# The first ordinary slab of the next product, token block by token block inside the norm

## The chip, the cores and the metric

The kernel runs on one core of one Trainium2 chip. The metric is the device time of one launch in microseconds (us). A core has five engines with an instruction queue each: TensorE (PE, matrix products), VectorE (DVE), ScalarE (ACT), GpSimd (POOL), and SyncE (SP), which here only issues loads. Each engine takes its instructions in the order of its queue; between engines, semaphores order the work.

## The reference, cut to what matters

256 tokens of width 1024 pass through a chain of blocks in float32. After each block comes a residual and a layer norm, and the next block begins with a product of the normalized x:

```python
def first_block(x, mem, ...):
    ...
    y = jnp.concatenate([mix, mem_out], axis=-1) @ w_out
    x = layer_norm(DN_ALPHA * x + y, ln_mix_g, ln_mix_b)              # norm 1
    h = jnp.square(jax.nn.relu(x @ w_up))
    return layer_norm(DN_ALPHA * x + h @ w_down, ln_ffn_g, ln_ffn_b)  # norm 2

def second_block(x, ...):
    for i in range(2):                    # i = 0: mla, i = 1: hyena
        m = mla_mixer(x, ...) if i == 0 else hyena_mixer(x, ...)
        x = layer_norm_2(ALPHA * x + m, ln1_g[i], ln1_b[i])           # norms 3 and 5
        x = layer_norm_2(ALPHA * x + conv_ffn(x, ...), ln2_g[i], ln2_b[i])  # norm 4 and the last
    return x

def conv_ffn(x, w_up, w_conv, w_down):
    h = dwconv_centred(x @ w_up, w_conv)
    a, g = jnp.split(h, 2, axis=-1)
    return (jax.nn.silu(g) * a) @ w_down
```

`first_block` is followed by `second_block`. The products that follow the five inner norms are: x @ w_up (norm 1), x @ mla_w_in (norm 2), x @ ffn_w_up of layer 0 (norm 3), x @ hy_w_in (norm 4), x @ ffn_w_up of layer 1 (norm 5).

## The kernel before

**Numbers.** Every large product is computed from parts: an fp32 operand is a high part in fp32r plus a low part (the difference), and three products (high by high, high by low, low by high) are summed in PSUM. `split` (L65 to L68) makes the parts: ACT copies the high part, DVE subtracts. The lines that the profile shows for it are L67 (ACT) and L68 (DVE).

**Weights.** `weights` (from L75) loads a slab of 128 x 1024 numbers, 512 KB, from SP's queue (L82) into one of three raw buffers, `wraw`, and splits it into `whi` (ACT) and `wlo` (DVE), of which there are five pairs. A raw buffer is free again after its `wlo`. So a load starts when the wlo of the slab three loads earlier is done.

**A product of weights by x** yields columns on the partitions and the 256 tokens along the free axis. `gemm_b` (L102) takes 24 matmuls of 256 columns for a slab, 8 each for (whi, x high), (wlo, x high), (whi, x low). After norm 1, `gemm_wide` (L110, L112) takes 8 matmuls of 512 columns (x high and low side by side) and 8 of 256.

**The norm.** A block's last product is summed in four PSUM banks, `acc`: two token blocks of 128 tokens by two halves of 512 columns (L116 to L118). `Down.end` writes the transition out by hand for each norm. Its parts are: `tail(b)`, the last matmuls of token block b; `ln_block(b, ...)`, the norm of the block on DVE (L159 to L170, with one small step on POOL) followed by transposes of the normalized rows on TensorE (`ln_t`, L178) and the split of the result into `x` (ACT, then DVE); `first_mm(b, ...)`, the product of this token block with the next weights' first 512 columns (L199, 24 matmuls of 512 columns, out of the four slabs `first`), written out to `utok` by ACT (L201). Later `first_pair` transposes `utok` (L209, `f4t`).

The order written by hand is tail(0), the norm of block 0, the four slabs of the first columns, tail(1), first_mm(0), the norm of block 1, first_mm(1). After that, `norm["after"] = 6` makes the splits of the next six slabs (in `weights`) come no earlier than the last DVE instruction of block 1's norm. A scheduler then sets the order on each engine from this program order and its own estimates of when things are ready; the engines keep that order.

The next stage then begins with an ordinary slab: `ff1_mm(4)`, `c_mm(4)`, `up(2)` (twice) or `hy_mm(4)`. It is followed by the products already at hand in `utok`.

**Side work.** During the first feed-forward stage `rope_tables` loads `posi` and casts it on DVE. During the first conv_ffn stage `hyena_filter` loads `f_wfb`, combines it on POOL into `f_wpm`, which ACT and DVE split into `f_wh` and `f_wl`.

Of the kernel before, what the change touches and what calls it, by code (L numbers as in the profile page):

```python
# [18 lines left out]
P = 128  # L19
# [24 lines left out]
def block_kernel(ctx, tc, A, out, taps=None):  # L44
# [11 lines left out]
    def bank(name="ps"):  # L56
        return psp.tile([P, 512], F32, name=name, tag="ps")
# [130 lines left out]
    def first_mm(b, x, ws, utok):  # L188
# [11 lines left out]
                             start=i == 0, stop=i == len(seq) - 1)  # L200
        nc.scalar.activation(utok[:, b, :], ps, AF.Copy)  # L201

    def first_pair(utok, i, ps=None):

        ps = bank("f4t") if ps is None else ps
        for j in range(2):
            for b in range(2):
                c = (2 * i + j) * P
                nc.tensor.transpose(ps[:, j * S + b * P:j * S + (b + 1) * P], utok[:, b, c:c + P], ident)  # L209
        return ps[:, :S], ps[:, S:]  # L210
# [3 lines left out]
    class Down:  # L214
# [21 lines left out]
                for i, (act, w) in enumerate(self.pend):  # L236
                    gemm_a(self.acc, b, h, act, w, False, i == len(self.pend) - 1)

        def end(self, gb, alpha, first, room=None):
            last = first is None  # L240
            x = utok = ws = None
            self.tail(0)
            if not last:
                x = new_x()
                utok = lnp.tile([P, 2, 512], F32, name="utok", tag="utok")
            ln_block(0, self.acc, x, gb, alpha, last)
            if not last:
                room = room or [None] * 4
                ws = [weights(first[i], room[i]) for i in range(4)]
            self.tail(1)  # L250
            if not last:
                first_mm(0, x, ws, utok)
            with tc.issue_after(norm["inst"].ins):
                ln_block(1, self.acc, x, gb, alpha, last)
            if not last:
                first_mm(1, x, ws, utok)
                norm["after"] = 6
            return x, utok

    def spare(pool, tags):  # L260

# [253 lines left out]
    pipeline([Stick(p) for p in range(SB_PAIRS)] + [Mem(p, b) for p in range(2) for b in range(2)], filler)  # L515
    for k in range(4, 8):
        u_dn(k)
    x, utok = dn.end(gb, ALPHA_1, A["w_up_f"], spare(p1, F4_TAGS))
    ph.close()
    tap("t_mix")  # L520

# [72 lines left out]
        nc.vector.tensor_copy(f_hl[0:64], hx[0:64].bitcast(F32))  # L594

    mlp = filter_mlp()
    ready = [ff1_act(ff1_mm(4))]
    order = [4, 0, 1, 2, 3] + list(range(5, FF1_TILES))
    for i in range(2):
        for ps in first_pair(utok, i):  # L600
# [1 line left out]
    for i in range(FF1_TILES):  # L602
# [4 lines left out]
            rope_tables()  # L607
        if i >= 6 and i % 4 == 2:
            next(mlp, None)
    x, utok = dn.end(gb, ALPHA_1, A["mla_w_in_f"], spare(p2, F4_TAGS))  # L610
    ph.close()
    tap("t_ffn")

# [29 lines left out]
        nc.vector.scalar_tensor_tensor(cl[:, nt, :], ps, gqk[:, nt:nt + 1], ch[:, nt, :].bitcast(F32),  # L643
                                       op0=ALU.mult, op1=ALU.subtract)

    c4 = c_mm(4)
    fp = [ps for i in range(2) for ps in first_pair(utok, i)]
    for j in range(3):
        c_act(j, fp[j])
# [125 lines left out]
    pipeline([Latent(h) for h in range(MLA_HEADS)], filler)  # L775
    for k in range(4, 8):
        u_wo(k)
    x, utok = dn.end(gb, ALPHA_2, A["ffn_w_up_f"][0], spare(p3, F4_TAGS))
    ph.close()
    rs.close()  # L780
    tap("t_mla")
# [82 lines left out]
        return steps + [(load_dft, "c_inv1"), (load_dft, "c_inv2")]  # L864


    def conv_ffn(layer, x, utok, nxt, side):
        with ExitStack() as es:
            pf = es.enter_context(tc.tile_pool(name=f"pf{layer}", bufs=1))
            todo = side(es.enter_context(tc.tile_pool(name="flt", bufs=1))) if side else []  # L870
            per = -(-len(todo) // (FF2_TILES - 5))
            wc = lnp.tile([P, 2 * FF2_TILES, 3], F32, name="wc", tag="wc")
            nc.sync.dma_start(wc, A["ffn_w_conv"][layer])
            gb = ln_load(pf, A["ln2_g"][layer], A["ln2_b"][layer])
            dn = Down(FF2_TILES, TAIL if nxt is not None else SPLIT_BUFS)

            def mm(nt):
                w = weights(A["ffn_w_up"][layer, nt])
                ps = bank("up")
                gemm_b(ps[:, :S], w, 0, x, KT)  # L880
                return ps[:, :S]

            def act(j, pss):
                ts = []
                for i in range(2):
                    t = pf.tile([P, S], F32, name=f"t{i}", tag=f"t{i}", bufs=2)
                    dwconv(t, pss[i], wc[:, j + i * FF2_TILES, :])
                    ts.append(t)
                ta, tg = ts
                nc.scalar.activation(tg, tg, AF.Silu)  # L890
                nc.vector.tensor_tensor(ta, ta, tg, op=ALU.mult)
                return act_split(pf, ta, "h", 5)

            def up(j):
                return act(j, [mm(2 * (j - 2) + i) for i in range(2)])

            ready = [up(2)]
            ready += [act(j, first_pair(utok, j)) for j in range(2)]
            order = [2, 0, 1] + list(range(3, FF2_TILES))
            for i in range(FF2_TILES):  # L900
                if i + 3 < FF2_TILES:
                    ready.append(up(i + 3))
                dn.add(ready[i], A["ffn_w_down"][layer, order[i]])
                if i:
                    for f, *a in todo[(i - 1) * per:i * per]:
                        f(*a)
            return dn.end(gb, ALPHA_2, nxt)

    x, utok = conv_ffn(0, x, utok, A["hy_w_in_f"], hyena_filter)
    tap("t_l0")  # L910


# [301 lines left out]
```

## Time and profile before

| what | us |
| --- | --- |
| median of 3 runs | 965.04 |
| lowest and highest run | 963.87, 969.01 |
| the profiled execution | 964.65 |
| its span in the trace | 962.9 |

The granted TensorE clock of the profiled execution is 0.992 on average. The table of the span in 40 slices shows the busy share in tenths:

```profile
PE   9999999999999999999999999998989999999996
DVE  6887679777667879779889788889779878777776
ACT  4676636454445577556666566445675355555551
```

TensorE is near full almost everywhere, DVE around three quarters, ACT about half. Times in the timeline are microseconds from the span's start; a row gives start, duration, engine, line, operation, out<-in, shapes, the count, and in brackets the idle time before it and what ended it. The five norms lie at about 122 to 141, 308 to 327, 400 to 419, 612 to 634 and 757 to 777 us.

### The profile page before, as it was taken

To read this page: it belongs to the slowest core of one execution; us is meant where nothing else is said; L and a number is where in the kernel's file an instruction comes from. 1 tells how busy PE (TensorE), PEld (TensorE's weight loads), DVE (VectorE), ACT (ScalarE), POOL (GpSimd) and SP (SyncE) were. 2 spreads that over 40 slices of the span, in tenths; PEclk is the share of its full clock that TensorE was granted. 3 is DMA by queue.
4 is the path that set the end of the run, shared out by engine and by line. 5 is a ranking of instruction groups with operands and counts; after the bars stand their busy time and mean duration, and the time that the engine had idled before them with its cause. 6 is when DMAs were issued, how large, how long until landed. Compare 5 with 4: busy or idle time off the path is not lost.

```text
span 962.9 us, 15208 instructions
## 1 busy us (share of the span) xinstructions
PE 932.9 (97%) x5808; PEld 823.7 (86%) x5808; DVE 761.1 (79%) x1201; ACT 539.9 (56%) x878; POOL 64.0 (7%) x61
## 2 busy tenths in 40 slices
PE   9999999999999999999999999998989999999996
PEld 6889788888887898788899999888978799999995
DVE  6887679777667879779889788889779878777776
ACT  4676636454445577556666566445675355555551
POOL 0000000000000010011312211001210000000000
PEclk9999999999999999999999999999989999999999
DMA  7764536655665443576555556436995565555551
GB/s 248 261 198 132 166 117 223 204 175 181 192 193 193 160 126 109 176 248 220 184 170 177 176 182 198 153 98 159 262 242 144 173 231 184 181 192 185 186 177 44
DMA packets 51082, 173.83 MB, mean 181 GB/s; under 512 B 6236, under 2 KB 7101, under 8 KB 50881
## 3 DMA queue, kind: packets, MB, share of 16 engines
q1 hardware_dynamic: 48656, 164.34, 52.6%
q0 software_dynamic: 2352, 8.52, 4.6%
q8 instruction: 46, 0.75, 0.3%
q14 instruction: 28, 0.22, 0.1%
HBM read 171.13 MB, written 1.05 MB: 179 GB/s over the span
## 4 chain that ended last, share of the span: by engine, by line
PE 75%; DVE 11%; DMA 7%; ACT 4%; issue 2%; SPq 0%; DVEq 0%; ACTq 0%; POOLq 0%
PE up L102 23%; PE acc L116 9%; PE acc L117 9%; PE acc L118 9%; PE up L110 5%; PE f L199 5%; DVE wlo L68 3%; PE up L112 3%; PE proj L102 2%; DMA wraw<-w_v 1%; ACT whi L67 1%; DMA wraw<-hy_w_in 1%; DMA wraw<-ffn_w_up_f 1%; PE hin L102 1%; DMA wraw<-w_qk 1%
## 5 line engine op out<-in xcount | busy, mean ns | idle before, releaser
L68 DVE TENSOR_TENSOR wlo<-wraw,whi 128x1024 fp32r<-128x1024 f32 (+1 forms) x255 | 310.4, 1220 | 78.4 <-ACT whi L67 77.5
L67 ACT ACTIVATE whi<-wraw 128x1024 fp32r<-128x1024 f32 (+1 forms) x255 | 265.2, 1044 | 128.1 <-PE acc L117 45.8
L102 PE MATMUL up<-x,whi 128*128 128x256 f32 x1280 | 173.7, 283 | 2.0 <-DVE t L790 2.0
L102 PEld LDWEIGHTS up<-x,whi 128*128 128x128 f32 x1280 | 164.8, 191 | 6.2 <-ACT whi L67 2.1
L118 PE MATMUL acc<-wlo,hh 128*128 128x512 f32 x304 | 119.9, 396 | 0.0
L116 PE MATMUL acc<-whi,hh 128*128 128x512 f32 x304 | 119.9, 396 | 0.0
L117 PE MATMUL acc<-whi,hl 128*128 128x512 f32 x304 | 119.9, 395 | 0.0
L102 PE MATMUL up<-x,wlo 128*128 128x256 f32 x640 | 89.8, 283 | 0.0
L787 ACT ACTIVATE t<-up,wc 128x256 f32<-128x256 f32 x80 | 37.7, 473 | 91.8 <-PE up L102 89.0
L102 PEld LDWEIGHTS up<-x,wlo 128*128 128x128 f32 x640 | 82.4, 192 | 0.0
L788 DVE SCALAR_TENSOR_TENSOR t<-up,wc,t 128x255 f32<-128x255 f32 x80 | 38.2, 479 | 46.3 <-ACT t L787 46.0
L118 PEld LDWEIGHTS acc<-wlo,hh 128*128 128x128 f32 x304 | 57.1, 188 | 13.5
L116 PEld LDWEIGHTS acc<-whi,hh 128*128 128x128 f32 x304 | 57.4, 189 | 11.3 <-ACT hh L67 0.5
L117 PEld LDWEIGHTS acc<-whi,hl 128*128 128x128 f32 x304 | 57.0, 188 | 11.0 <-DVE hl L68 0.3
L110 PE MATMUL up<-x,whi 128*128 128x512 f32 x224 | 56.6, 395 | 0.0
L165 POOL TENSOR_TENSOR ln_rs<-ln_rs,mhalf 128x1 f32<-128x1 f32 x12 | 11.5, 958 | 646.3 <-DVE ln_rs L164 646.3
L110 PEld LDWEIGHTS up<-x,whi 128*128 128x128 f32 x224 | 41.8, 188 | 10.6 <-issue 1.1
L102 PE MATMUL hin<-x,whi 128*128 128x256 f32 x320 | 46.7, 292 | 0.0
L102 PEld LDWEIGHTS hin<-x,whi 128*128 128x128 f32 x320 | 42.7, 199 | 0.3
L790 DVE SCALAR_TENSOR_TENSOR t<-up,wc,t 128x255 f32<-128x255 f32 x80 | 38.3, 480 | 2.1
L67 ACT ACTIVATE hh<-h 128x256 fp32r<-128x256 f32 x32 | 13.1, 415 | 39.1 <-DVE h L544 38.0
L112 PEld LDWEIGHTS up<-x,wlo 128*128 128x128 f32 x224 | 30.6, 190 | 2.3
(404 smaller groups left out, 1665.2 us busy)
## 6 DMA issues: line engine op xcount, KB each, us to landing
wraw<-ffn_w_up SPq DMA_DIRECT2D x80, 512.0 KB, 4.2
wraw<-ffn_w_down SPq DMA_DIRECT2D x44, 512.0 KB, 3.7
wraw<-w_down SPq DMA_DIRECT2D x32, 512.0 KB, 3.5
wraw<-w_up SPq DMA_DIRECT2D x28, 512.0 KB, 4.3
wraw<-hy_w_in SPq DMA_DIRECT2D x20, 512.0 KB, 5.1
wraw<-w_qk SPq DMA_DIRECT2D x14, 512.0 KB, 4.5
wlo<-hy_w_in POOLq DMA_DIRECT2D x11, 512.0 KB, 9.4
wraw<-w_out SPq DMA_DIRECT2D x8, 512.0 KB, 3.4
```

Source lines behind the costliest of these rows:

```text
L67: nc.scalar.activation(hi, src, AF.Copy)
L68: nc.vector.tensor_tensor(lo, src, hi.bitcast(F32), op=ALU.subtract)
L102: nc.tensor.matmul(ps, a[:, off + k * P:off + (k + 1) * P], m[:, k, :], start=i == 0, stop=i == len(seq) - 1)
L110: nc.tensor.matmul(ps, wh[:, k * P:(k + 1) * P], xx[:, k], start=k == 0, stop=False)
L112: nc.tensor.matmul(ps[:, :S], wl[:, k * P:(k + 1) * P], xh[:, k, :], start=False, stop=k == KT - 1)
L116: nc.tensor.matmul(ps, ah, mh, start=start, stop=False)
L117: nc.tensor.matmul(ps, al, mh, start=False, stop=False)
L118: nc.tensor.matmul(ps, ah, ml, start=False, stop=stop)
L199: nc.tensor.matmul(ps, x[xi][:, k, tb], ws[k // 2][wi][:, o:o + 512], start=i == 0, stop=i == len(seq) - 1)
L787: norm["act"] = nc.scalar.activation(dst, ps, AF.Copy, scale=w3[:, 1:2])
L788: nc.vector.scalar_tensor_tensor(dst[:, 1:], ps[:, :S - 1], w3[:, 0:1], dst[:, 1:], op0=ALU.mult, op1=ALU.add)
L790: norm["dve"] = nc.vector.scalar_tensor_tensor(dst[:, :S - 1], ps[:, 1:S], w3[:, 2:3], dst[:, :S - 1], op0=ALU.mult, op1=ALU.add)
```

## The change

Each of the five callers hands `end` one more slab, `lead`: the one that its stage took first. `end` loads it right behind the four slabs of the first columns, and `lead_mm` multiplies it with one token block at a time, directly after `first_mm` of that block: 24 matmuls of 128 columns for block 0, ahead of block 1's transposes, and 24 for block 1. The result is one PSUM bank of 256 columns, `lead`, that the stage uses in place of its first product. The count of slabs whose splits are held back becomes 5, since one slab fewer follows. After norm 1, `ff1_act` gets a product of 256 columns in place of the wide one, and so takes its other branch.

```diff
+    def lead_mm(ps, b, x, w):
+        tb = slice(b * P, (b + 1) * P)
+        seq = [(w[i], x[j], k) for i, j in ((0, 0), (0, 1), (1, 0)) for k in range(KT)]
+        for i, (a, m, k) in enumerate(seq):
+            nc.tensor.matmul(ps[:, tb], a[:, k * P:(k + 1) * P], m[:, k, tb],
+                             start=i == 0, stop=i == len(seq) - 1)
...
-        def end(self, gb, alpha, first, room=None):
+        def end(self, gb, alpha, first, lead=None, room=None):
...
                 ws = [weights(first[i], room[i]) for i in range(4)]
+                lw = weights(lead)
             self.tail(1)
             if not last:
+                ps = bank("lead")
                 first_mm(0, x, ws, utok)
+                lead_mm(ps, 0, x, lw)
             with tc.issue_after(norm["inst"].ins):
                 ln_block(1, self.acc, x, gb, alpha, last)
             if not last:
                 first_mm(1, x, ws, utok)
-                norm["after"] = 6
-            return x, utok
+                lead_mm(ps, 1, x, lw)
+                norm["after"] = 5
+                ps = ps[:, :S]
+            return x, utok, ps
...
-    x, utok = dn.end(gb, ALPHA_1, A["w_up_f"], spare(p1, F4_TAGS))
+    x, utok, lead = dn.end(gb, ALPHA_1, A["w_up_f"], A["w_up"][0], spare(p1, F4_TAGS))
-    ready = [ff1_act(ff1_mm(4))]
+    ready = [ff1_act(lead)]
...
-    x, utok = dn.end(gb, ALPHA_1, A["mla_w_in_f"], spare(p2, F4_TAGS))
+    x, utok, c4 = dn.end(gb, ALPHA_1, A["mla_w_in_f"], A["mla_w_in"][0], spare(p2, F4_TAGS))
-    c4 = c_mm(4)
...
-    x, utok = dn.end(gb, ALPHA_2, A["ffn_w_up_f"][0], spare(p3, F4_TAGS))
+    x, utok, lead = dn.end(gb, ALPHA_2, A["ffn_w_up_f"][0], A["ffn_w_up"][0, 0], spare(p3, F4_TAGS))
-            ready = [up(2)]
+            ready = [act(2, [lead, mm(1)])]
...
-            return dn.end(gb, ALPHA_2, nxt)
+            return dn.end(gb, ALPHA_2, nxt, nxt_lead)
...
-    va = [hy_mm(4)]
+    va = [lead]
```

The calls at norm 4 (`A["hy_w_in"][0]`) and norm 5 (`A["ffn_w_up"][1, 0]`) change in the same way.

How this moves instructions is shown at norm 1. On ACT, with the buffer numbers, before the change, from the last slab split ahead of the norm to the write of `utok` of block 1 (`x` from `ln_t_1423` and `ln_t_1431` is block 0, the next pair block 1):

```order
L67 ACTIVATE whi_1673<-wraw_1672 128x1024
L67 ACTIVATE x_1408<-ln_t_1423 128x4x128
L67 ACTIVATE x_1408<-ln_t_1431 128x4x128
L201 ACTIVATE utok_1409<-f4_1478 128x512
L67 ACTIVATE x_1408<-ln_t_1517 128x4x128
L67 ACTIVATE x_1408<-ln_t_1525 128x4x128
L67 ACTIVATE whi_1695<-wraw_1694 128x1024
L67 ACTIVATE whi_1726<-wraw_1725 128x1024
L201 ACTIVATE utok_1409<-f4_1532 128x512
```

And the same place of the changed kernel, where `wraw_1454` is lead's slab, loaded ahead of `wraw_1672`:

```order
L67 ACTIVATE whi_1704<-wraw_1703 128x1024
L67 ACTIVATE x_1408<-ln_t_1423 128x4x128
L67 ACTIVATE x_1408<-ln_t_1431 128x4x128
L67 ACTIVATE whi_1726<-wraw_1725 128x1024
L201 ACTIVATE utok_1409<-f4_1485 128x512
L67 ACTIVATE whi_1757<-wraw_1756 128x1024
L67 ACTIVATE x_1408<-ln_t_1548 128x4x128
L67 ACTIVATE x_1408<-ln_t_1556 128x4x128
L201 ACTIVATE utok_1409<-f4_1563 128x512
```

Two splits of slabs, 1726 and 1757, that stood behind x of block 1 now stand ahead of it. At norms 2 and 3 one such split does (`whi_3522` of w_uq_n, `whi_4656` of ffn_w_down); at norms 4 and 5 none stands between utok of block 0 and x of block 1.

On DVE, before the change, from the end of block 1's norm at norm 1 to the cast of `posi`:

```order
L170 SCALAR_TENSOR_TENSOR xt<-xt,ln_rs,ln_b 128x512 x2
L68 TENSOR_TENSOR wlo<-wraw,whi 128x1024 x2
L68 TENSOR_TENSOR x<-ln_t,x 128x4x128 x2
L68 TENSOR_TENSOR wlo<-wraw,whi 128x1024 x4
L543 TENSOR_TENSOR h<-up,h 128x256
L540 TENSOR_TENSOR h<-h 128x256
L544 SCALAR_TENSOR_TENSOR h<-h 128x256
L68 TENSOR_TENSOR hl<-h,hh 128x256 x2
L68 TENSOR_TENSOR wlo<-wraw,whi 128x1024
L540 TENSOR_TENSOR h<-h 128x256 x2
L68 TENSOR_TENSOR hl<-h,hh 128x256 x2
L558 CAST ang<-posi 128x256
```

And of the changed kernel:

```order
L170 SCALAR_TENSOR_TENSOR xt<-xt,ln_rs,ln_b 128x512 x2
L68 TENSOR_TENSOR wlo<-wraw,whi 128x1024 x4
L68 TENSOR_TENSOR x<-ln_t,x 128x4x128 x2
L571 CAST ang<-posi 128x256
L68 TENSOR_TENSOR wlo<-wraw,whi 128x1024
L553 TENSOR_TENSOR h<-h 128x256 x2
L572 TENSOR_SCALAR ang<-ang,invf 128x256
L68 TENSOR_TENSOR hl<-h,hh 128x256 x2
```

The cast moved ahead of the first h. On SP, the loads of this place before the change:

```order
L82 DMA wraw<-w_down 128x1024
L150 DMA ln_g<-ln_ffn_g 128x1024
L150 DMA ln_b<-ln_ffn_b 128x1024
L82 DMA wraw<-w_up 128x1024
L82 DMA wraw<-w_down 128x1024
L554 DMA posi<-positions 128x256
```

And of the changed kernel:

```order
L82 DMA wraw<-w_down 128x1024
L82 DMA wraw<-w_up 128x1024
L150 DMA ln_g<-ln_ffn_g 128x1024
L150 DMA ln_b<-ln_ffn_b 128x1024
L567 DMA posi<-positions 128x256
```

One slab more is issued ahead of ln_g, and posi follows ln_b directly.

More of the change, by code (lines that the diff above doesn't have):

```diff
@@ L237, in tail @@
                     gemm_a(self.acc, b, h, act, w, False, i == len(self.pend) - 1)
-        def end(self, gb, alpha, first, room=None):
+        def end(self, gb, alpha, first, lead=None, room=None):
             last = first is None
-            x = utok = ws = None
+            x = utok = ws = lw = ps = None
             self.tail(0)
@@ L864, in hyena_filter, with conv_ffn @@
         return steps + [(load_dft, "c_inv1"), (load_dft, "c_inv2")]
-    def conv_ffn(layer, x, utok, nxt, side):
+    def conv_ffn(layer, x, utok, lead, nxt, nxt_lead, side):
         with ExitStack() as es:
@@ L906, in conv_ffn @@
                         f(*a)
-            return dn.end(gb, ALPHA_2, nxt)
-    x, utok = conv_ffn(0, x, utok, A["hy_w_in_f"], hyena_filter)
+            return dn.end(gb, ALPHA_2, nxt, nxt_lead)
+    x, utok, lead = conv_ffn(0, x, utok, lead, A["hy_w_in_f"], A["hy_w_in"][0], hyena_filter)
     tap("t_l0")
@@ L1091, in block_kernel @@
     room = keep.tile([P, 4, 2, D], F32R, name="Kf", tag="Kf")
-    x, utok = dn.end(gb, ALPHA_2, A["ffn_w_up_f"][1], [(room[:, i, 0], room[:, i, 1]) for i in range(4)])
+    x, utok, lead = dn.end(gb, ALPHA_2, A["ffn_w_up_f"][1], A["ffn_w_up"][1, 0], [(room[:, i, 0], room[:, i, 1]) for i in range(4)])
     ph.close()
     tap("t_hy")
-    conv_ffn(1, x, utok, None, None)
+    conv_ffn(1, x, utok, lead, None, None, None)
 def _tiles(w):
```

## The prediction

> **What bounds the kernel now.** I read the head of the page first, then the table of what TensorE (PE) waited for, then busy time by stretch around the five norms.
>
> ```profile
> span 962.9 us, 15208 instructions
> PE 932.9 (97%) x5808; PEld 823.7 (86%) x5808; DVE 761.1 (79%) x1201; ACT 539.9 (56%) x878; POOL 64.0 (7%) x61
> ...
> PE ln_t L178 <- DVE xt L170: 2.1, 2, 1.1
> PE f L199 <- ACT x L67: 0.9, 3, 0.3
> ```
>
> TensorE is busy 97% of the span, so a microsecond that TensorE loses or gains counts nearly in full. At the norms it waits little: 2.1 us for the normalized rows and 0.9 us for the split of x (and once 0.7 us for utok, in a row further down). These 3.7 us are all that work put between the first columns and the transposes could fill.
>
> ```profile
> 128.00:150.00 22.00, 21.70 (x110) 18.09 (x109) 17.21 (x26) 8.56 (x16) 0.99 (x1) 1.00 0.53 187
> 312.00:331.00 19.00, 17.99 (x100) 15.01 (x101) 15.75 (x27) 8.31 (x19) 1.15 (x2) 1.00 0.33 110
> 331.00:403.00 72.00, 70.78 (x454) 62.94 (x453) 57.76 (x130) 50.39 (x106) 4.47 (x7) 1.00 0.51 161
> 403.00:433.00 30.00, 29.70 (x187) 26.32 (x186) 24.81 (x36) 15.35 (x24) 3.33 (x4) 1.00 0.58 196
> 618.00:640.00 22.00, 20.10 (x116) 16.82 (x116) 17.88 (x27) 9.25 (x13) 0.99 (x1) 1.00 0.46 142
> 640.00:763.00 123.00, 113.66 (x734) 102.94 (x733) 104.99 (x157) 73.42 (x108) 14.11 (x16) 0.96 0.74 197
> 763.00:785.00 22.00, 21.64 (x132) 18.54 (x131) 17.10 (x25) 8.88 (x13) 0.92 (x1) 1.00 0.48 164
> ```
>
> The columns are the window, its length, and busy time of PE, weight loads, DVE, ACT, POOL. The idle of PE (length less busy) is 0.3 us at norm 1, 1.0 at norm 2, 0.3 at norm 3, 1.9 at norm 4 (window from 618), 0.4 at norm 5; the stage after norm 2 has 1.2 and the hyena stage (640 to 763) 9.3.
>
> **The price of the matmuls.** The chain that ended last gives spacings:
>
> ```profile
> 141.37 1.85 PE up L110 x8
> 143.23 0.95 PE up L112 x8
> ...
> 327.19 2.88 PE c L102 x24
> ...
> 371.26 1.05 PE o L760 x4
> ```
>
> An fp32r matmul of 512 columns costs 231 ns (1.85 / 8), one of 256 columns 119 to 120 ns (0.95 / 8; 2.88 / 24). The product that the change replaces costs 2.8 us at norm 1 and 2.88 us at the others. In its place stand 2 x 24 matmuls of 128 columns. No fp32r matmul below 256 columns is in the trace. Lower bound: 60 ns, half of 120, if only columns count. Upper bound: 216 ns, the plain fp32 matmul of 256 columns (the row of o: 3 spacings and one duration of 0.386 us make 1.05). The nearest row of the same width is that of the fp32 transposes:
>
> ```profile
> 134.20 1.03 PE L178 MATMUL ln_t<-ident,xt 128*128 128x128 f32 x8
> 135.54 1.21 PE L199 MATMUL f<-f4h,x 128*128 128x512 f32 x4 [0.30 <-ACT x L67]
> ```
>
> Eight take 1.03 us with the last one's own 0.276 us, so (1.03 - 0.28) / 7 = 108 ns. I take 115 ns, between this and the 120 ns at 256 columns, which means that halving the columns gains nearly nothing while the weights are loaded anew each time. Then 24 cost 2.76 us, a norm's two 5.5 us, 2.7 us more than before.
>
> [...]
>
> **Norm 1: the split of block 1 comes behind a load.** The instruction order shows the main step. Before the change ACT does x (block 1) right after utok; now whi of raw 1756 stands between them. The three raw buffers go round: 1454 (lead), 1672, 1703, then 1725 in lead's buffer and 1756 in that of 1672, whose wlo is the first that DVE does after block 1's norm. So this load starts after the norm. These rows of ACT, DVE and SP of before show how long this takes:
>
> ```profile
> 134.89 1.08 ACT L67 ACTIVATE x<-ln_t 128x512 fp32r<-128x512 f32 x2
> 139.32 1.06 ACT L67 ACTIVATE whi<-wraw 128x1024 fp32r<-128x1024 f32 x1 [3.35 <-DMA wraw<-w_up]
> ...
> 132.24 1.41 DVE L170 SCALAR_TENSOR_TENSOR xt<-xt,ln_rs,ln_b 128x512 f32<-128x512 f32 x2
> 133.56 2.35 DVE L68 TENSOR_TENSOR wlo<-wraw,whi 128x1024 fp32r<-128x1024 f32 x2
> ...
> 134.85 0.33 SPq L82 DMA_DIRECT2D wraw<-w_up  x1
> ```
>
> The norm of block 1 ends at about 133.6, the first wlo at 134.8, SP issues the load at 134.85, and ACT can split it at 139.32; before, x was long done and this hurt nobody. Now the load in this slot is w_down, of the same size. x of block 1 starts at 139.32 + 1.06 = 140.4 and f of block 1, which started 0.65 us after x (134.89, 135.54), at 141.0: 5.4 us late. Behind the waiting whi on ACT stand both x and utok; TensorE has only lead(0) (2.8 us) and the transposes for that time, then idles about 2.5 us. lead(1) ends at 141.0 + 5.7 + 2.76 = 149.4, where up(4) ended at 144.0, so 5.4 us are lost by then. On DVE the added wlo inside block 0's norm (1.2 us) fits in an idle of the same size there; I cost it at nothing, and at 1.2 us if that cover is gone.
>
> Then a second one. The cast of posi moves on DVE from behind four hl to right behind x, ahead of the first h:
>
> ```profile
> 146.04 0.44 SPq L554 DMA_DIRECT2D posi<-positions  x1
> ...
> 151.74 0.30 DVE L558 CAST ang<-posi 128x256 f32<-128x256 int32 x1 [0.57 <-DMA posi<-positions]
> ...
> 147.71 0.39 PE L116 MATMUL acc<-whi,hh 128*128 128x512 f32 x1
> ```
>
> The load took 5.7 us. On SP it now stands behind the loads of ln_g and ln_b, which wait for the end of f of block 1 (146.6): issue about 147.7, landing 153.4. Behind the cast on DVE are wlo, h and hl, for which acc waits: 153.4 + 0.3 + 1.2 + 0.4, and the hi and lo parts, gives acc at about 155.7, where it began at 147.71. **Norm 1: +8.0 us.**
>
> **Norm 2**, the same trap:
>
> ```profile
> 312.95 0.63 PE L178 MATMUL ln_t<-ident,xt 128*128 128x128 f32 x4 [0.98 <-DVE xt L170]
> ...
> 320.44 1.22 DVE L68 TENSOR_TENSOR wlo<-wraw,whi 128x1024 fp32r<-128x1024 f32 x1
> ...
> 324.89 0.85 ACT L67 ACTIVATE whi<-wraw 128x768 fp32r<-128x768 f32 x1 [2.95 <-DMA wraw<-w_uq_r]
> ```
>
> Here lead's wlo inside block 0's norm is not hidden, since the transposes already waited 0.98 us for DVE: +1.2 us. The first wlo after block 1's norm moves from 320.44 to 321.7; 4.45 us after its start the loaded slab was split (324.89), so now at 326.1, for 0.85 us. f of block 1 starts at 327.6 instead of 321.32 (0.65 us after x). It ends at 333.4, lead(1) at 336.1; c ended at 327.19 + 2.88, about 329.9 with the overlap of the last. **+6.2 us.** lead(0), from 321.2, is hidden.
>
> **Norm 3**, the same again, with POOL behind it:
>
> ```profile
> 411.86 2.35 DVE L68 TENSOR_TENSOR wlo<-wraw,whi 128x1024 fp32r<-128x1024 f32 x2
> ...
> 413.05 1.08 ACT L67 ACTIVATE x<-ln_t 128x512 fp32r<-128x512 f32 x2
> 416.86 1.06 ACT L67 ACTIVATE whi<-wraw 128x1024 fp32r<-128x1024 f32 x1 [2.73 <-DMA wraw<-ffn_w_up]
> ...
> 432.33 0.64 ACT L67 ACTIVATE f_wh<-f_wpm 128x512 fp32r<-128x512 f32 x1 [0.76 <-POOL f_wpm L827]
> ...
> 434.57 0.63 ACT L67 ACTIVATE f_wh<-f_wpm 128x512 fp32r<-128x512 f32 x1 [1.30 <-POOL f_wpm L827]
> ...
> 439.59 1.19 PE L102 MATMUL up<-x,whi 128*128 128x256 f32 x8 [1.82 <-DVE t L790]
> ```
>
> The wlo moves from 411.86 to 413.1, the whi from 416.86 to 418.1, x to 419.2, f to 419.8, from 413.70 (413.05 + 0.65): 6.1 us; with the narrower product 6.2 at the end of lead(1). After that ACT has both f_wh ahead of t of the second product; their input comes from POOL at 432.3 and 434.6 before, and at about 433.8 and 436 now, since its load is issued about 1.4 us later. The t of the second product is then read at about 436.6, over 11 us later than before, its bank is not free, and acc begins some 4 us later than the 6.2 alone explain. Of this, 1.8 us come back, because the wait of 1.82 us at 439.59 came from the same filter work. **+8 us** (6.2 to 10).
>
> **Norm 4**: x of block 1 stands ahead of the late whi, so there is no trap.
>
> ```profile
> 625.74 0.44 PE L209 MATMUL f4t<-ident,utok 128*128 128x128 f32 x2 [0.69 <-ACT utok L201]
> 627.30 1.38 PE L178 MATMUL ln_t<-ident,xt 128*128 128x128 f32 x8 [1.12 <-DVE xt L170]
> ```
>
> lead(0) fills the two waits (1.8 us), but one more wlo stands ahead of block 1's norm on DVE, so the transposes go from 627.3 to 628.5. **+1.1 us** (1.2 and lead(1) for the old product, 2.76 for 2.88).
>
> **Norm 5**: no trap either (block 1's x comes first), but nothing hides: block 0's norm ended when the transposes began, so its added wlo costs 1.2 us.
>
> ```profile
> 761.98 1.41 DVE L170 SCALAR_TENSOR_TENSOR xt<-xt,ln_rs,spec_q 128x512 f32<-128x512 f32 x2
> ...
> 763.24 1.03 PE L178 MATMUL ln_t<-ident,xt 128*128 128x128 f32 x8
> ```
>
> With the 2.7 us of narrower matmuls, less 0.1: **+3.8 us.**
>
> Sum: 8.0 + 6.2 + 8.0 + 1.1 + 3.8 = 27.1; I take off 1 us for what the idle of 1.2 us after norm 2 gives back. 964.65 (the profiled execution: span 962.9 and 1.75 around it) + 26 = 990.7; the median of the runs is 0.4 above that execution: **991 us.**
>
> **Rivals.**
> - *The late whi costs less than its row.* If these loads land before the norm's end (another slot free sooner), f of block 1 starts on time, and what is left is the narrow matmuls and the wlo: norm 1 +2.7, norm 2 +3.9, norm 3 +3.3, norm 4 +1.1, norm 5 +3.8, or 980. For it: at 139.32 the wait was for a load, not for ACT. Against it: the load cannot start before its buffer is free. Chance 0.15.
> - *Later stages take it back.* The hyena stage has 9.3 us of idle PE, part of it for loads whose issue need not move with TensorE. If the stage starts 23 us late with weights landed, up to 9 us return: 982. Against it: its buffers are freed by the same delayed engines. Chance 0.12.
> - *The reordered hyena stage, or a matmul of up to 216 ns, costs more.* At 216 ns lead(1) costs 2.4 us more at each norm, and at norm 5 and part of norm 4 lead(0) too: about +15, or 1006. Chance 0.10.
> - *Faster than before.* The waits that work can fill are 1.8 us at norm 4 and about 0.4 elsewhere, 2.2 in all. They are a gain if the late whi and the added wlo hide entirely and a matmul of 128 columns takes less than 69 ns (5 x (48 x 0.069 - 2.88) = 2.2); at 60 ns the time is about 963. Below 960 there is nothing to gain. Chance 0.04.
> - *The narrow matmul is cheap.* At the lower bound of 60 ns the traps remain and lead(0) stays hidden at norms 1 to 4: lead(1) saves 24 x 0.055 = 1.3 us at five norms, lead(0) as much at norm 5, 983. For it: columns set the 231 and 120 ns. Against it: the 108 ns of the transposes. Chance 0.04. [...]
>
> The forecast keeps 0.55.
>
> **Range.** The forecast alone spans 983 to 999 (matmul at 60 to 120 ns, norm 3 at +6.2 to +10, the hyena stage by a few us). I reach below to the two cases of 980 and 982, with some for both together, and above toward 1006: 974 to 1003. A difference under 0.5% cannot be told from none for this kernel, by the spread of its runs. Slower by more than that 0.93, within it 0.04, faster 0.03.
>
> **What would show it.** A wait of f for ACT x of 2 us and more at norms 1, 2 and 3, and none at 4 and 5; on ACT a whi that waits some 3 us for its load right ahead of x of block 1; the lead rows at about 115 ns each; DVE waiting for posi ahead of the first h; acc 8 us late at norm 1. It is wrong if f of block 1 starts as promptly as before.

## The result, and the profile after

| what | us |
| --- | --- |
| after, median of 6 runs (lowest to highest) | 1004.42 (1000.72 to 1009.59) |
| before on the same chip, median of 6 runs | 964.45 |
| ratio, with its 95% interval | 1.041 (1.0383 to 1.0438) |
| the profiled execution after, and its span | 1004.86, 1003.1 |

The kernel became 40 us slower, where 26 were forecast; 1004.42 lies just above the range, which ended at 1003. The mean granted clock of the profiled execution is 0.981 (0.992 before).

The head of the page after, with the busy time by engine:

```profile
span 1003.1 us, 15462 instructions
PE 954.4 (95%) x5936; PEld 843.5 (84%) x5936; DVE 759.8 (76%) x1200; ACT 540.2 (54%) x878; POOL 62.2 (6%) x61
```

TensorE (PE) works 21.5 us longer than before (954.4 for 932.9) and idles 18.7 us longer (1003.1 - 954.4 = 48.7, against 30.0). What it waited for, after (us in total, times, longest):

```profile
PE f L199 <- ACT x L67: 8.2, 6, 2.6
PE hin L102 <- DMA wlo<-hy_w_in: 6.1, 4, 4.6
PE y L116 <- ACT g L799: 4.0, 1, 4.0
PE hyt L947 <- issue: 3.9, 1, 3.9
PE up L102 <- ACT t L799: 3.4, 1, 3.4
```

The first row, 0.9 us before, is the one that the forecast named. The waits of hin, y and hyt stand in the hyena stage, of which the forecast expected nothing; before the change hin waited 3.7 us for such loads, y 2.7 and hyt 2.6.

**Where the time was lost.** Both programs have 1320 matmuls into `acc`, in the same order. The start of the n-th of them after, less its start before, is the delay so far; its growth over a stage is what the stage lost. It is read to 0.1 us from the two profiled executions. The last column is for the version of experiment 6, which is taken up below. lead(0) and lead(1) are the products of the new slab with token block 0 and block 1.

| stage | forecast | after | experiment 6 |
| --- | --- | --- | --- |
| norm 1 | +8.0 | +8.6 | +2.6 |
| norm 2 | +6.2 | +5.1 | +4.9 |
| norm 3 and the first conv_ffn stage | +8.0 | +13.9 | +6.3 |
| norm 4 and the hyena stage | +1.1 | +9.1 | -0.9 |
| norm 5 | +3.8 | +3.5 | +3.0 |
| all (the forecast less 1 for an idle) | +26 | +40.2 | +15.9 |

Three stages came out within 1.1 us of the forecast. Two did not: norm 3 with its stage, and norm 4 with the hyena stage, by 5.9 and 8.0 us.

**Norm 1.** Rows of the timeline after, in groups of PE, ACT and DVE:

```profile
134.09 1.90 PE L208 MATMUL lead<-x,whi 128*128 128x128 f32 x16
135.83 1.06 PE L208 MATMUL lead<-x,wlo 128*128 128x128 f32 x8
140.17 1.19 PE L199 MATMUL f<-f4h,x 128*128 128x512 f32 x4 [2.38 <-ACT x L67]
154.35 0.50 PE L116 MATMUL acc<-whi,hh 128*128 128x512 f32 x1 [2.05 <-ACT hh L67]
...
138.57 1.06 ACT L67 ACTIVATE whi<-wraw 128x1024 fp32r<-128x1024 f32 x1 [3.68 <-DMA wraw<-w_down]
139.54 1.07 ACT L67 ACTIVATE x<-ln_t 128x512 fp32r<-128x512 f32 x2
...
152.09 0.29 DVE L571 CAST ang<-posi 128x256 f32<-128x256 int32 x1 [10.00 <-DMA posi<-positions]
```

On ACT the split whi waits 3.68 us for its load, x of block 1 stands behind it, and f starts at 140.17 (forecast 141.0) after an idle of 2.38 us (about 2.5). The cast of posi holds DVE until 152.4, and acc starts at 154.35 (155.7). A narrow matmul took (135.83 - 134.09) / 16 = 109 ns; 115 was taken.

**Norm 3.** PE after; in experiment 3, below, the same 4 matmuls of f take 1.08 us:

```profile
433.08 2.07 PE L199 MATMUL f<-f4h,x 128*128 128x512 f32 x4 [2.65 <-ACT x L67]
434.95 1.91 PE L199 MATMUL f<-f4l,x 128*128 128x512 f32 x4
...
454.38 2.05 PE L102 MATMUL up<-x,whi 128*128 128x256 f32 x8 [3.38 <-ACT t L799]
456.22 1.91 PE L102 MATMUL up<-x,wlo 128*128 128x256 f32 x8
...
467.98 1.18 PE L102 MATMUL up<-x,whi 128*128 128x256 f32 x8 [1.55 <-DVE t L802]
```

The waits are there, as forecast. But behind the first two the same matmuls take almost twice their time (4 of f 1.91 us for 1.08, 8 of up 1.91 for 1.12). Three stretches after, with the columns of the windows quoted ahead of the result (the third number from the end is the granted clock):

```profile
140.00:146.00 6.00, 5.83 (x27) 4.80 (x27) 2.09 (x3) 0.60 (x2) 0.00 (x0) 1.00 0.36 125
155.00:159.00 4.00, 4.00 (x12) 3.15 (x13) 4.00 (x12) 2.86 (x7) 0.00 (x0) 0.62 0.46 138
433.00:439.00 6.00, 5.92 (x14) 4.66 (x15) 2.00 (x3) 0.52 (x2) 0.00 (x0) 0.50 0.47 168
```

From 433 to 439 TensorE worked at half its clock: 14 matmuls in 6 us. Its busy share is near full there, and shows nothing of it. From 140 to 146, behind the idle of 2.38 us, the clock is full.

**The hyena stage.** DVE after, from the first short convolution `u`; then PE after; then PE at the same place before:

```profile
668.69 1.23 DVE L68 TENSOR_TENSOR wlo<-wraw,whi 128x1024 fp32r<-128x1024 f32 x1 [2.07 <-ACT whi L67]
669.83 0.48 DVE L797 TENSOR_SCALAR u<-f4t,ws 128x256 f32<-128x256 f32 x1
671.32 1.23 DVE L68 TENSOR_TENSOR wlo<-wraw,whi 128x1024 fp32r<-128x1024 f32 x1 [1.01 <-ACT whi L67]
672.47 0.48 DVE L800 SCALAR_TENSOR_TENSOR u<-f4t,ws,u 128x255 f32<-128x255 f32 x1
...
666.26 1.20 PE L102 MATMUL hin<-x,whi 128*128 128x256 f32 x8
673.56 0.48 PE L947 MATMUL hyt<-ident,u 128*128 128x128 f32 x2 [3.94 <-issue]
```

```profile
637.67 1.20 PE L102 MATMUL hin<-x,whi 128*128 128x256 f32 x8
640.63 0.41 PE L935 MATMUL hyt<-ident,u 128*128 128x128 f32 x2
```

The first `hin` of the stage starts 28.6 us later than before (666.26, 637.67), of which 27.6 were lost by norm 3: norm 4 itself costs 1.0 us. But the first transpose `hyt` of u follows 7.3 us behind it, where it was 3.0. On DVE two wlo whose slabs are late stand among the u that hyt waits for.

### The profile page after: what moved, and what is told of

Read it like the earlier page. It is cut to its first block, busy times and chain, and to the rows that moved or that the text cites. A ratio compares the mean times of both kernels' runs of the same rounds, so it can differ in the third digit from the quotient of the medians.

```text
span 1003.1 us, 15462 instructions
## 1 busy us (share of the span) xinstructions
PE 954.4 (95%) x5936; PEld 843.5 (84%) x5936; DVE 759.8 (76%) x1200; ACT 540.2 (54%) x878; POOL 62.2 (6%) x61
## 3 DMA queue, kind: packets, MB, share of 16 engines
HBM read 171.13 MB, written 1.05 MB: 172 GB/s over the span
## 4 chain that ended last, share of the span: by engine, by line
PE 67%; DVE 12%; DMA 12%; ACT 5%; issue 3%; POOL 0%; SPq 0%; DVEq 0%; ACTq 0%; POOLq 0%
PE up L102 21%; PE acc L116 7%; PE acc L117 7%; PE acc L118 7%; PE up L110 5%; PE f L199 4%; DVE wlo L68 3%; PE up L112 2%; PE proj L102 2%; DMA wraw<-hy_w_in 2%; PE hin L102 2%; ACT whi L67 2%; DMA wraw<-ffn_w_up 1%; DMA wraw<-w_qk 1%; DVE ln_st L160 1%
## 5 line engine op out<-in xcount | busy, mean ns | idle before, releaser
L102 PE MATMUL up<-x,whi 128*128 128x256 f32 x1248 | 171.4, 285 | 4.9 <-ACT t L799 3.4
L102 PEld LDWEIGHTS up<-x,whi 128*128 128x128 f32 x1248 | 162.3, 193 | 8.9 <-ACT t L799 3.6
L102 PEld LDWEIGHTS up<-x,wlo 128*128 128x128 f32 x624 | 81.1, 193 | 0.0
L116 PEld LDWEIGHTS acc<-whi,hh 128*128 128x128 f32 x304 | 57.7, 190 | 13.6 <-ACT hh L67 2.8
L118 PEld LDWEIGHTS acc<-wlo,hh 128*128 128x128 f32 x304 | 57.3, 188 | 13.6
L110 PEld LDWEIGHTS up<-x,whi 128*128 128x128 f32 x216 | 40.6, 189 | 10.4 <-issue 1.1
L102 PE MATMUL hin<-x,whi 128*128 128x256 f32 x304 | 44.4, 293 | 0.0
L199 PE MATMUL f<-f4h,x 128*128 128x512 f32 x96 | 27.4, 419 | 7.7 <-ACT x L67 7.6
```

Source lines behind the costliest of these rows:

```text
L102: nc.tensor.matmul(ps, a[:, off + k * P:off + (k + 1) * P], m[:, k, :], start=i == 0, stop=i == len(seq) - 1)
L110: nc.tensor.matmul(ps, wh[:, k * P:(k + 1) * P], xx[:, k], start=k == 0, stop=False)
L116: nc.tensor.matmul(ps, ah, mh, start=start, stop=False)
L118: nc.tensor.matmul(ps, ah, ml, start=False, stop=stop)
L199: nc.tensor.matmul(ps, x[xi][:, k, tb], ws[k // 2][wi][:, o:o + 512], start=i == 0, stop=i == len(seq) - 1)
```

## The experiments

Each change is to the changed kernel unless something else is said. Medians are of 4 runs (12 for experiment 8), each with the ratio to the kernel before on the same chip (964.85 us for experiments 1 to 4, 966.53 for 5 to 8, 964.14 for 9 and 10); the kernel before itself differs by up to 2.4 us between these, so a difference of medians from two groups is uncertain by as much. Losses by stage are read as in the table above, from the profiled execution of each; in experiments 1, 2 and 4 that was the slowest of the four (4.7, 2.9 and 3.3 us above the median), so that its stages add up to more.

### 1. The late splits behind x on ACT

The splits that are held back until block 1's norm are also held behind x of block 1 on ACT.

```diff
-        nc.scalar.activation(hi, src, AF.Copy)
+        norm["split"] = nc.scalar.activation(hi, src, AF.Copy)
...
+                es.enter_context(tc.issue_after(norm["x"].ins))
...
+            norm["x"] = norm["split"]
```

> The whole change, but the splits that were held back behind the norm on DVE are also held back on ACT, behind the split of x of block 1. Theory (the split of x of block 1 waits behind a slab's split whose load starts after the norm): the waits of f for ACT x at norms 1 to 3 fall from 2.4, 1.8 and 2.7 us to about 0.3, the half-speed stretch at norm 3 goes, and what is left is the narrow matmuls (48 x 0.109 - 2.88 = 2.4 us a norm), the added wlo (0.8 at norms 2 and 3), 9 us at norm 4 and in the hyena stage, 3.5 at norm 5: about 986 (982 to 990). Rival (the 48 narrow matmuls and their place are the cost, however ACT is ordered): 1000 or more.

Measured: **989.93 us** (987.69 to 994.64), ratio 1.0256 (1.0236 to 1.0276). ACT and PE of this kernel at norm 1:

```profile
137.97 1.09 ACT L67 ACTIVATE x<-ln_t 128x512 fp32r<-128x512 f32 x2 [2.49 <-PE ln_t L179]
138.94 2.95 ACT L67 ACTIVATE whi<-wraw 128x1024 fp32r<-128x1024 f32 x3
...
138.62 1.20 PE L201 MATMUL f<-f4h,x 128*128 128x512 f32 x4 [0.25 <-ACT x L67]
```

x now comes right behind its transposes, and f waits 0.25 us in place of 2.38. The order on ACT is worth 1004.42 - 989.93 = 14.5 us. Norm 1 costs 2.9 us instead of 8.6; the late acc went with the late f. Norm 2 hardly gained (4.4 for 5.1), norm 3 with its stage costs 8.8 for 13.9. The hyena stage stays as bad (10.9 with norm 4).

### 2. The slab of lead in one piece

`lead` is multiplied after the first columns of both blocks, in 24 matmuls of 256 columns; its load and its splits stay early.

```diff
-                lead_mm(ps, 0, x, lw)
...
-                lead_mm(ps, 1, x, lw)
+                gemm_b(ps[:, :S], lw, 0, x, KT)
```

> The slab is loaded early as in the change and its splits stand in the same place, but its product is one piece of 24 matmuls of 256 columns behind the first columns of block 1. Theory (late splits and narrow matmuls): here ACT does x of block 1 ahead of the late splits, so the three traps and the narrow matmuls go; what is left is the wlo inside block 0's norm, about 1 us at norms 2, 3 and 5, and whatever the hyena stage makes of its new order: 966 to 977. Rival (loading and splitting a fifth slab ahead of the norm is the cost): about 1000.

Measured: **970.82 us** (968.44 to 973.69), ratio 1.0067 (1.0043 to 1.0091), as expected. Norm 1 costs nothing at all, norm 2 +2.9, norm 3 +3.6, hyena +2.0. Taking lead(0) from between the blocks gives back most of the loss, more than its 24 matmuls of 109 ns at each norm come to: with it goes the order, since f of block 1 now starts at 135.47 at norm 1 after a wait of 0.30 us. This run alone does not tell the matmuls from the order. Experiment 10, which adds the restored orders to it, takes the same time (970.85), so with the slab in one piece they gain nothing more.

### 3. Work in the idle ahead of f

8, 6 and 9 matmuls of 512 columns, whose result nothing reads, between the transposes and f of block 1 at norms 1, 2 and 3. They leave the orders of ACT and DVE and keep TensorE from idling.

```diff
+                if fill:
+                    dummy = acc_bank(0, 0, "fill")
+                    with tc.issue_after(norm["t"].ins):
+                        for _ in range(fill):
+                            nc.tensor.matmul(dummy, x[0][:, 0, :P], ws[0][0][:, :512], start=True, stop=True)
```

> The whole change, with 8, 6 and 9 matmuls of 512 columns of no use between the transposes and the first columns of block 1 at norms 1, 2 and 3, 0.23 us each, less than TensorE idled there. Theory (after idle of more than 2 us TensorE runs at half its clock for some us): the first columns of block 1 at norm 3 run at full clock, 2.9 us less, and the rest stays: about 1001. Rival (the half clock has nothing to do with the idle): 1004 or more.

Measured: **1000.32 us** (997.12 to 1001.89), ratio 1.0367 (1.0344 to 1.0391). PE at norm 3, and the same stretch of the clock:

```profile
431.01 2.33 PE L271 MATMUL fill<-f4h,x 128*128 128x512 f32 x9
433.99 1.21 PE L199 MATMUL f<-f4h,x 128*128 128x512 f32 x4 [0.66 <-ACT x L67]
435.04 1.08 PE L199 MATMUL f<-f4l,x 128*128 128x512 f32 x4
...
433.00:439.00 6.00, 5.34 (x24) 4.12 (x23) 2.42 (x3) 1.43 (x3) 0.00 (x0) 1.00 0.59 212
```

f cannot start earlier, since x comes no earlier, but the clock is 1.00 in place of 0.50, and 4 matmuls take 1.08 us in place of 1.91. f takes 5.63 us (433.99 to 439.62) instead of 8.45 (433.08 to 441.53). The half clock, not the data, was the rest of what f lost at norm 3; the norm with its stage costs 10.0 us for 13.9. The gain in time, 4.1 us by the medians, is of the size of the runs' spread (1000.72 to 1009.59 without the filling); the rows show it more plainly.

### 4. The change at norm 4 alone

The other four norms get no `lead` and keep their old order (norm 1 shown, the others alike).

```diff
-    x, utok, lead = dn.end(gb, ALPHA_1, A["w_up_f"], A["w_up"][0], spare(p1, F4_TAGS))
+    x, utok, lead = dn.end(gb, ALPHA_1, A["w_up_f"], None, spare(p1, F4_TAGS))
...
-    ready = [ff1_act(lead)]
+    ready = [ff1_act(ff1_mm(4))]
```

> The change at norm 4 alone; the other four norms as before. Theory (the hyena stage is made longer by its own new instruction order): 1 us at the norm and 8 in the stage, about 973. Rival (the stage only suffers from what the norms before it left behind, or norm 4 gains its two filled waits): 962 to 966.

Measured: **977.72 us** (975.43 to 981.06), ratio 1.014 (1.0115 to 1.0165). Norms 1 to 3 cost next to nothing here (1.5 us in all), and norm 4 with the hyena stage costs 13.6. The wait ahead of hyt is there too:

```profile
648.93 0.67 PE L951 MATMUL hyt<-ident,u 128*128 128x128 f32 x2 [3.65 <-issue]
```

So the loss in that stage comes from the change there, and does not follow from a late start. The 13.6 are read from the slowest execution; by the median this whole version costs 12.9 us. That the stage loses more than the 9.1 us in the full change is not from more waiting: from norm 4 to shortly before norm 5 (620.59 to 776.90 us here, 646.69 to 798.52 in the full change, 619.08 to 761.84 before) TensorE idles 17.9 us here, 17.7 in the full change and 11.3 before. The granted clock of the same stretches is 0.92, 0.96 and 0.96.

### 5. The hyena stage's order on DVE

The splits of the two slabs that follow `hy_mm(7)` are held behind the last u that reads `f4t`; the hold from norm 4 ends there.

```diff
+    norm["u"] = norm["dve"]
+    norm["after"] = 0
...
+    norm["inst"], norm["after"] = norm["u"], 2
```

> The whole change, but in the hyena stage the splits of the slabs behind hy_mm(7) are held back on DVE behind the last u made from f4t, which gives DVE the order it had there before the change. Theory (a wlo that waits for its load stands ahead of the u that TensorE waits for, and TensorE then runs the next us at half clock): the wait of 3.9 us ahead of hyt goes, the stage gives back most of its 8 us: about 997 (995 to 999). Rival (the narrow matmuls or the earlier fifth load disturb the stage's loads): 1003 to 1005.

Measured: **996.24 us** (995.77 to 996.49), ratio 1.0319 (1.0296 to 1.0342). DVE, then PE of this kernel:

```profile
666.41 0.48 DVE L797 TENSOR_SCALAR u<-f4t,ws 128x256 f32<-128x256 f32 x1
...
666.14 1.20 PE L102 MATMUL hin<-x,whi 128*128 128x256 f32 x8
669.10 0.41 PE L947 MATMUL hyt<-ident,u 128*128 128x128 f32 x2
```

hyt follows hin by 3.0 us again, with no wait, and the stage with norm 4 costs 1.5 us instead of 9.1. The order on DVE is the cause.

### 6. Both orders

Experiments 1 and 5 together.

> The whole change with both orders restored: the splits held back on ACT behind x of block 1, and the hyena stage's on DVE behind u. Theory (the waits are all a matter of order, and add up): 990 from the run with the first alone, less 7: about 983; the matmuls are still narrow and lead(0) still in place, 5 x 2.4 = 12 us of it. Rival (order explains little of what is left): 988 or more.

Measured: **980.30 us** (977.88 to 981.09), ratio 1.015 (1.0126 to 1.0175). The two orders together are worth 24.1 of the 40 us (1004.42 - 980.30), or 26.2 if each is taken against its own kernel before. What is left, 15.9 in the trace, is spread over the norms (last column of the table). At norm 2 the restored order brings a new wait: f no longer waits for x (0.25 us), but qr, a product of the next stage, waits 1.51 us for an ACT instruction, and 0.89 us in experiment 1.

### 7. The rope tables later

`rope_tables`, with the cast of posi, is called some slabs later.

```diff
-        if i == 3:
+        if i == 8:
```

> The whole change, with rope_tables called behind the ninth slab of the first feed-forward stage instead of the fourth; on DVE the cast of posi then stands behind the first two h and hl. Theory (DVE is stuck on the load of posi, TensorE waits 2 us for it and then loses 2 us at a reduced clock): acc of the first feed-forward stage starts about 2 us earlier and runs at full clock, 4 us less: about 1000. Rival (acc waits for the late x alone): 1004.

Measured: **998.57 us** (996.35 to 1000.04), ratio 1.0342 (1.0316 to 1.0368). PE of this kernel at norm 1:

```profile
139.08 1.20 PE L199 MATMUL f<-f4h,x 128*128 128x512 f32 x4 [2.30 <-ACT x L67]
...
152.66 0.39 PE L116 MATMUL acc<-whi,hh 128*128 128x512 f32 x1
```

The wait of 2.05 us ahead of acc is gone, and from 155 to 159 us the clock is 1.00 instead of 0.62. The delay behind norm 1 is 5.0 us instead of 8.6. In this execution the last acc ahead of the norm came 1.1 us earlier than before the change, so the norm itself costs 6.1. Of this, 1.6 us are a half clock of f (to 146.33, 7.25 us for 5.66), which the full change did not have at this place. Without these two, the gain is near the 4 us expected: the cast is the second half of the forecast for norm 1.

### 8. The idles of the kernel before, filled

In the kernel before, matmuls whose result nothing reads at four places of its hyena stage where TensorE idles, to see whether a steadier clock alone gains.

```diff
+        if nt in (12, 19):
+            for k in range(KT):
+                nc.tensor.matmul(ps[:, :S], w[0][:, k * P:(k + 1) * P], x[0][:, k, :], start=k == 0, stop=k == KT - 1)
...
+            if nt0 == 6 and i == 0:
+                with tc.issue_after(norm["pe"].ins):
+                    for _ in range(8):
+                        nc.tensor.matmul(tp, norm["w"][0][:, :P], norm["w"][0][:, :512], start=True, stop=True)
...
```

> The kernel before, with matmuls of no use in three of the places where TensorE idles in the hyena stage: 8 of 512 columns ahead of a transpose of u that waits 2.6 us, 8 of 256 columns ahead of the products of slabs 12 and 19, and 7 of 512 ahead of the second y1, which waits 2.2 us. Theory (idle time makes the following us run at half clock): the stage loses less of its clock and ends 2 to 4 us earlier, so 961 to 963, faster than both kernels. Rival (the loads of the stage set its end, and a faster TensorE only waits longer for them): 964 to 967.

Measured: **965.22 us** (962.86 to 967.27), ratio 0.9991 (0.9974 to 1.0008): no gain. The stage's clock hardly moved (0.97 from 640 to 763 us, 0.96 before), and other waits came up: 2.8 us of hyt for a split on ACT.

### 9. More idles of the changed kernel filled

Experiment 3, with 7 more such matmuls ahead of the first acc behind norm 1 and 12 ahead of the second product behind norm 3.

```diff
-    dn = Down(FF1_TILES)
+    dn = Down(FF1_TILES, fill=7)
...
+                if layer == 0 and nt == 3:
+                    dummy = acc_bank(1, 1, "fill")
+                    with tc.issue_after(norm["pe"].ins):
+                        for _ in range(12):
+                            nc.tensor.matmul(dummy, w[0][:, :P], w[0][:, :512], start=True, stop=True)
```

> The kernel of the first filled run (matmuls of no use ahead of the first columns of block 1 at norms 1 to 3), with 7 more ahead of acc behind norm 1, where TensorE waited 2.05 us, and 12 more behind norm 3 ahead of the up that waited 3.4 us. Every engine but TensorE keeps its order and its waits. Theory (what follows these two waits ran at a reduced clock because TensorE had idled): the 2.0 us lost behind the first and the 2.4 us behind the second come back, so 4 us less than that run's 1000.3: about 996. Rival (the reduced clock comes from elsewhere, and more matmuls only add work): 1000 or more.

Measured: **1001.33 us** (1000.69 to 1001.8), ratio 1.038 (1.0366 to 1.0395). In sum, the rival's number. In its trace the two places differ; a window and PE of this kernel:

```profile
456.00:462.00 6.00, 6.00 (x27) 5.14 (x28) 5.76 (x12) 4.38 (x9) 0.00 (x0) 0.72 0.72 254
...
450.71 1.19 PE L102 MATMUL up<-x,whi 128*128 128x256 f32 x8 [2.14 <-ACT t L809]
456.00 0.50 PE L117 MATMUL acc<-whi,hl 128*128 128x512 f32 x1 [1.45 <-DVE hl L68]
```

At norm 1 the clock stays at 1.00 (from 155 to 159 us). The delay behind the norm is 5.5 us instead of experiment 3's 8.5, but 1.3 us of this were gained ahead of the norm; the norm itself costs 6.8, which is 1.7 less, where 2.0 were expected. At norm 3 there is still a wait of 2.14 us behind the 12 matmuls. The products behind it run at full speed (8 matmuls in 1.19 us), but acc then waits another 1.45 us, and only behind that does the clock fall (0.72): 11.9 us there against 10.0. The hyena stage costs 10.1 us against 6.7 in experiment 3, although nothing was changed in it. Its granted clock was 0.94 for 0.97, which over some 150 us is worth 3 to 4 us by estimate, and so most of the difference.

### 10. Both orders, and lead in one piece

Experiments 6 and 2 together: early slab and splits, orders restored, no narrow matmuls.

> Both orders restored, as in the run at 980.3, and the early slab's product in one piece of 24 matmuls of 256 columns behind the first columns of block 1 instead of 48 of 128 columns. Theory (a matmul of 128 columns costs nearly one of 256): 5 x 2.4 = 12 us less, plus about 2 us for the waits at norm 4 that lead(0) had filled: about 970. Rival (the narrow matmuls cost little, what is left is the early load and its wlo): 976 to 980.

Measured: **970.85 us** (968.85 to 974.65), ratio 1.0069 (1.0045 to 1.0094). Against experiment 6 the narrow matmuls, together with lead(0)'s place ahead of the transposes, are worth 980.30 - 970.85 = 9.5 us, or 7.1 if each is taken against its own kernel before; the two traces differ by 9.4 us. The groups of lead in the two kernels (busy time, mean ns of one, idle time), experiment 6 first:

```profile
L210 PE MATMUL lead<-x,whi 128*128 128x128 f32 x160 | 19.0, 272 | 0.0
L210 PE MATMUL lead<-x,wlo 128*128 128x128 f32 x80 | 10.6, 275 | 0.0
```

```profile
L103 PE MATMUL lead<-x,whi 128*128 128x256 f32 x80 | 11.2, 283 | 0.0
L103 PE MATMUL lead<-x,wlo 128*128 128x256 f32 x40 | 5.6, 283 | 0.0
```

240 narrow matmuls are busy for 29.6 us and 120 of twice the width for 16.8: 12.8 us more work, of which 9.5 show in the time. Idles do not hide the rest: TensorE idles 32.7 us in experiment 6 and 32.8 here. All its matmuls together are busy only 9.5 us less here (936.6 for 946.1), since this execution's granted clock was lower (0.987 for 0.991; over 940 us that makes 3.8 by estimate, for the 3.3 that lack). With the orders restored and no narrow matmul the kernel is still 0.7% above the kernel before; no version of the change was faster.

## Why the prediction was right, and where it was wrong

The forecast was 991 us, in a range up to 1003; measured were 1004.42. The mechanism that it named is there, and two steps of its sum failed: norm 3 without a slow clock, and the hyena stage at nothing.

The 40 us, taken apart by the medians: both orders 24.1 (experiment 6), the narrow matmuls and lead(0)'s place 9.5 (experiment 10), and 6.4 that are left. With each version against its own kernel before they are 26.2, 7.1 and 6.7. Of what is left, 4.6 lie at norm 3 and the stage behind it (delays of experiment 10): acc waits 1.63 and 2.13 us there, and the granted clock from 436 to 443 us is 0.51. The rest was not taken apart; the wlo ahead of block 1's norm is a likely part, since the transposes wait 4.5 us in all for the normalized rows in experiment 10, and 2.1 before the change.

**Right: the late whi on ACT.** The wait of f for x came up at norms 1, 2 and 3 as forecast, and experiment 1 removes it with this order alone; the waits were 2.38, 1.81 and 2.65 us, where 2 us and more were named. At norm 3 f of block 1 is 19.4 us late (433.08, 413.70), of which 13.7 were there before: 5.7, where 6.1 were forecast.

**Right: the cast of posi**, by experiment 7. That norm 1 came out at 8.6 for 8.0 is partly luck, two errors that cancel: acc started 6.6 us late (154.35, 147.71) where 8.0 were forecast, and the half clock then added 1.7, since the first 12 matmuls of acc took 4.46 us (to 158.81) in place of 2.8.

**Right: the narrow matmul**, 109 ns for 115, nearer to the transposes' 108 than taken. The rivals at 60 and at 216 ns fall (by its own row the upper bound is 221: 1.05 less 0.386, by 3).

**Right: norms 2, 4 and 5**, within 1.1 us.

**The rival "the late whi costs less than its row"**, 980 us, did not happen, but its price is what remains when the order is put right: 980.30 in experiment 6, with norm 5 at 3.0 for 3.8, norm 1 at 2.6 for 2.7, norm 2 at 4.9 for 3.9; norm 3, at 6.3 for 3.3, was mis-sized, and norm 4 with the hyena stage came out at -0.9 for 1.1. So the equal sum is partly luck.

**Wrong: norm 3, "+8 us (6.2 to 10)".** Of its steps, the late f (5.7 for 6.1) and the late second product (a wait of 3.38 us for "some 4") hold. Two things do not. "Of this, 1.8 us come back" fails: at that place 1.55 us are still waited for (the row at 467.98; 1.82 before). And the sum has no term for the clock: f of block 1 took 8.45 us where experiment 3's takes 5.63, +2.8; the 24 matmuls from 454.38 took 5.25 (to 459.63) where 24 take 2.88, +2.4. Together they are 5.2 of the 5.9 us that the forecast is short there. The 2.8 are shown by experiment 3. The 2.4 are read from rows: in experiment 9 the same matmuls run at full speed behind the filled wait, but the clock falls behind a later wait of acc (1.45 us; 0.72 from 456 to 462), and the stage gains nothing.

**Wrong: the hyena stage, taken at nothing.** The sum has no term for it, and the range only "a few us". Of the rivals, "later stages take it back" gave up to 9 us back; nothing came back, and the stage lost 8.1 us. "The reordered hyena stage" was named among the rivals, with a chance of 0.10, but its 1006 us were worked out from the matmul alone. The step that failed is that the instruction order was read only at the norms: on DVE two wlo had moved among the first u, and these u have a reader, hyt, that TensorE reaches 3 us into the stage. Experiment 5 shows it by putting the order back (1.5 us with norm 4), experiment 4 by having nothing else (13.6). Over the six versions with the new order there (the full change and experiments 1, 3, 4, 7 and 9) the loss ranges from 6.7 to 13.6 us, and it is larger where the granted clock over the stage is lower (0.97 in experiment 3, 0.92 in experiment 4). Slower loads alone are not the cause: the slabs of hy_w_in took 8.0 us to land in the median in experiment 5, 6.9 in the full change and 5.1 before, and the wait is gone in experiment 5 all the same.

The range was too narrow by these two: it gave the hyena stage "a few us" and the clock nothing.

## What to carry to other kernels

Moving one product earlier also moves its slab's load and splits, and every engine that takes its queue in order then passes the late slab's wait on to whatever stands behind it (at norm 1 a split on ACT waited 3.68 us for its load, and f 2.38 us for the x behind it); so read the new order on ACT and DVE through the whole following stage, not only at the edit, and look for an instruction that waits for a load ahead of one that TensorE needs soon. Where a forecast finds a new idle of some two microseconds on TensorE (in the full change 2.05, 2.65 and 3.38 us had slow matmuls behind them), add a term for a slow clock behind it, as a chance: at norm 1 an idle of 2.38 us cost nothing in one execution, and one of 2.30 us at the same place cost 1.6 us in another. Halving the columns of an fp32r matmul from 256 to 128 saved almost nothing here: 120 to 109 ns.

## What the hardware showed that was not expected

**The clock falls behind short idles, but not behind each.** After an idle of 2.65 us (norm 3) the granted clock was 0.50 for the next 6 us, and after 3.38 us 8 matmuls of 256 columns took 1.91 us, where 1.12 is usual; after 2.38 (norm 1) and 1.81 us (norm 2) 4 matmuls of f took 1.08 to 1.10 us, the full speed. After 2.05 us ahead of acc the matmuls took 0.40 us at 155.65 and 0.63 us from 156.25 on: the slow rows began only 1.5 us into the work, which starts at 154.35.

The trace shows when the clock changes. In the profiled execution of the change it falls from 1.00 to 0.50 at 39.88, 155.94, 432.42, 452.90, 674.76, 702.07, 743.03 and, at the end of the kernel, 999.03 us; the first seven times it is back at 1.00 after 3.41 us or 6.83 us. The falls lie 34, 81, 6, 65, 8, 12 and 75 times 3.41 us apart (3.413 in the trace). Windows between points of this spacing, of the full change and then, in the last two rows, of experiment 7:

```profile
138.87:142.29 3.42, 2.12 (x9) 1.78 (x10) 2.42 (x3) 1.74 (x3) 0.00 (x0) 1.00 0.51 190
152.53:155.94 3.41, 1.59 (x6) 1.10 (x7) 3.41 (x10) 1.88 (x4) 0.00 (x0) 1.00 0.31 74
155.94:159.35 3.41, 3.41 (x10) 2.64 (x9) 3.41 (x10) 2.27 (x6) 0.00 (x0) 0.50 0.43 118
...
136.72:140.13 3.41, 1.11 (x6) 0.88 (x6) 1.56 (x2) 2.03 (x3) 0.00 (x0) 1.00 0.84 317
140.13:143.54 3.41, 3.41 (x10) 2.67 (x9) 0.86 (x2) 0.00 (x0) 0.00 (x0) 0.50 0.48 154
```

The idle of 2.38 us is cut by such a point at 138.87 (29 times 3.41 us behind the first fall), 1.1 us lie ahead of it and 1.3 behind, and the clock stays at 1.00. The idle of 2.30 us at the same place in experiment 7 falls into one window, and the next one runs at 0.50. In the full change each fall of the clock follows a window in which TensorE idled 1.82 us or more, and no window at 1.00 with 1.73 us or less (667.94 to 671.35) is followed by one. In other runs the two kinds overlap: in the kernel before a window with 1.82 us of idle is followed by a fall (697.38 to 700.79) and another with 1.82 us is not (953.38 to 956.79), and in experiment 9 the fall at 457 follows waits of 0.26 and 1.45 us; three falls behind windows with only 0.75 to 1.12 us of idle (experiments 1, 4 and 9) stay open.

A window without any work is not needed for a fall: from 152.53 to 155.94 TensorE worked 1.59 of 3.41 us, and the clock was 0.50 in the next one. No run here was made to measure the border.

**Behind a filled idle the clock stayed full.** Behind 9 matmuls that left 0.66 us of idle it was 1.00 (433 to 439 us of experiment 3; 0.50 without them). Behind 12 that left 2.14 us (experiment 9) the next matmuls ran at full speed too, but the waits of the acc that followed, 0.26 and 1.45 us, were followed by a fall of the clock at 457.
